# Softmax denominators spread by transfers through DRAM, and convolution steps laid over thirteen units of attention, in a diffusion-transformer layer

## The chip, the cores and the metric

The kernel runs on one core of a Trainium2 chip. The core has five engines with a queue of instructions each: TensorE (PE; its weight loads are listed apart as PEld), VectorE (DVE), ScalarE (ACT), GpSimd (POOL) and SyncE (SP, which here only issues transfers). Each queue is worked off in the order in which it was built, and engines wait for each other by semaphores. The metric is the device time of one execution in microseconds (us); lower is better.

## The reference

One layer over 1024 latent tokens of width 1024 with a context of 256 tokens: a half-step gated feed-forward network (FFN), then a short gated convolution and an attention in parallel, merged by gates and a projection, then a second FFN. Everything is float32. The change is in the attention and in the convolution's projection `y_conv @ w_bc`, which runs beside it.

```python
def gqa_attend(q, k, v):
    s = jnp.einsum('btkgd,blkd->bkgtl', q, k, preferred_element_type=jnp.float32) * (HEAD_DIM ** -0.5)
    p = jax.nn.softmax(s, axis=-1).astype(v.dtype)
    return jnp.einsum('bkgtl,blkd->btkgd', p, v)

def merge_branches(y_conv, o_attn, gate_logits, w_bc, w_ba, w_out):
    g_conv, g_attn = jnp.split(jax.nn.sigmoid(gate_logits), 2, axis=-1)
    return (g_conv * (y_conv @ w_bc) + g_attn * (o_attn @ w_ba)) @ w_out
```

There are 8 query heads and 2 key/value heads of width 128. Each of the 1024 latent queries attends in one softmax to 256 context and 1024 latent keys.

## The kernel before

To keep float32 precision, a product is made of three matmuls of a faster 32-bit form (`fp32r`): each operand is split in a high part (an ACT copy, shown as CAST) and a low part (a subtraction on DVE or POOL), and high x high, high x low and low x high are summed (`mm3`).

Attention is cut in 16 `Unit`s: 8 heads by 2 chunks of 512 queries (`C0`, `C1`). A unit has four parts.

- `begin` splits its 512 queries into two tiles `qs`.
- `scores(qt)`, for four groups of 128 queries: three 256-wide matmuls `ps<-kc,qs` against the context keys and two times three 512-wide ones `ps<-kl,qs` against the latent keys, into `ps` banks of PSUM (5 banks). DVE takes the maximum of each piece (`m`) and of the three (`nm`), ACT exponentiates the pieces into SBUF (`pc`, `pl`, `pl`) and accumulates the row sums, and DVE adds these up (`rsum`).
- `turn(kt)`, for ten groups of 128 keys: four PE transposes `pt<-ident,pc` or `pt<-ident,pl` into one `pt` bank (2 banks), which is split to a pair of tiles `pts` (CAST on ACT, subtraction on DVE).
- `values(kt)`: three matmuls `po<-pts,...` that add up over the ten groups in `po`, of which there is one bank. `po` holds head dimension by queries, so the row sums, which lie one query to a partition, have to be turned and spread over all partitions before they can divide it. That is `output`, at the end of the unit: reciprocal `rinv` on DVE, four PE transposes of `rinv` (each column spread over 128 columns) into a `pt` bank, a copy of `po` to SBUF on ACT (`q<-po`), and a multiplication on DVE (`q<-q,pt`).

The main loop (L1635) runs for unit 1 to 15. It makes the scores of one unit, and between them it takes steps from two generators: `rest` (`seconds()`: the turns and values of all units in order, with values three groups behind the turns) and `fill` (`fillers()`: the convolution projection in steps of three matmuls `ps<-y,wc`, 107 yields with the loads of its weights and inputs). A `conv_out` loads its gate `g`, multiplies it with the result on DVE and stores it to DRAM as `zd`. Of ten `rest` steps in a unit, with n = 3, 2, 3, 2 between the scores, each is followed by a `fill` step until the fourth score is made, and each n = 2 gives one more: 3 + 3 + 3 + 1 = 10 fill steps for each unit, so that the fillers end in unit 11. `split_output` splits finished heads into `oh` and `ol` for the merge that follows.

The order on each engine isn't the order of this code alone: when the program is built, a scheduler places the instructions by its own estimate of times, with the order in the code as the priority (except where a load or matmul is `pinned`). Moving a step in the code can so move the whole queue. Tiles come from pools with a fixed number of buffers, and an instruction waits until the buffer it writes is free: `qs`, `g`, and other 512-wide tiles share 11 buffers named `t`. All engine instructions are recorded at one line (L88, a helper), so rows of the profile are told apart by the names of tiles.

Of the kernel before, what the change touches and what calls it, by code (L numbers as in the profile page):

```python
# [9 lines left out]
F32 = mybir.dt.float32  # L10
# [8 lines left out]
P = 128  # L19
# [30 lines left out]
def tile_dit_layer(  # L50
# [44 lines left out]
    act, dve, pool, pe, sp = (Engine(e) for e in (nc.scalar, nc.vector, nc.gpsimd, nc.tensor, nc.sync))  # L95
# [7 lines left out]
    dram = ctx.enter_context(tc.tile_pool(name="dram", bufs=1, space=DRAM))  # L103
# [3 lines left out]
    def uniq(s):  # L107
        n_tiles[0] += 1
        return f"{s}_{n_tiles[0]}"

    def atile(name, shape=(P, SLOT), dt=F32):
        return apool.tile(list(shape), dt, tag="A", name=uniq(name))

    def ttile(name, n=512, dt=F32):
        t = tpool.tile([P, 512], dt, tag="t", name=uniq(name))
        return t[:, :n]

    def small(name, n, dt=F32):
        return spool.tile([P, n], dt, tag=f"s{n}_{name}", name=uniq(name))

    def ps_s(n=512):
        return psum.tile([P, 512], F32, tag="s", name=uniq("ps"), bufs=5)[:, :n]

    def ps_t(n=512):
        return psum.tile([P, 512], F32, tag="t", name=uniq("pt"), bufs=2)[:, :n]
# [10 lines left out]
    def transpose(out, in_, pinned=False):  # L136
        n = in_.shape[0]
        inst = pe.transpose(out, in_, ident[:n, :n])
        if pinned:
            tc.keep_in_program_order(inst)  # L140
# [35 lines left out]
    def col(name, k=0):  # L176
        o = voff[name] + k
        return cols[:, o : o + 1]
# [40 lines left out]
    def mm3(ps, terms, k0=0, k1=None):  # L219

        last = len(terms) - 1
        for i, (wh, wl, xh, xl) in list(enumerate(terms))[k0:k1]:
            matmul(ps, wh, xh, start=(i == 0), stop=False)
            matmul(ps, wh, xl, start=False, stop=False)
            matmul(ps, wl, xh, start=False, stop=(i == last))
# [219 lines left out]
    def run(steps, n=None):  # L445

        if n is None:
            for _ in steps:
                pass
        else:  # L450
            for _ in range(n):
                next(steps, None)
# [541 lines left out]
    def turn(toks, k, pt):  # L994
        for j, t in enumerate(toks):
            transpose(pt[:, j * P : (j + 1) * P], t[:, k * P : (k + 1) * P])
# [25 lines left out]
    pr = ttile("pr")  # L1022
# [169 lines left out]
    for j in range(NH):  # L1192
        half1.side = side(j) if j >= SIDE_FROM else None
        u, c = half1.next_first()
        v, b = half1.second(u)
# [15 lines left out]
    for d in range(0, KD, 2):  # L1211
# [3 lines left out]
        for e in range(2):  # L1215
            te = t[:, e * CT : (e + 1) * CT]
            dve.scalar_tensor_tensor(
                out=te, in0=c_acc(d + e), scalar=gate1["c"][:, d + e : d + e + 1], in1=te, op0=ALU.mult, op1=ALU.add
# [71 lines left out]
    for i in range(KD):  # L1290
        u = atile("u")
# [5 lines left out]
        for ch, bg, gc in mixed():  # L1297
# [4 lines left out]
            for j in (0, 2):  # L1302
                a, b = max(o, 1 - j), min(o + 512, L + 1 - j)
                ya = y[:, a - o : b - o]
                dve.scalar_tensor_tensor(
                    out=ya, in0=u[:, a + j - 1 : b + j - 1], scalar=col(f"w{j}", i), in1=ya, op0=ALU.mult, op1=ALU.add
# [181 lines left out]
    def split_output(hd, *chunks):  # L1488
        if o_parts[hd] is None:
            o_parts[hd] = atile("oh", dt=F32R), atile("ol", dt=F32R)  # L1490
        a, b = chunks[0][1], chunks[-1][1] + 512
        split(q_f[hd][:, a:b], *(t[:, a:b] for t in o_parts[hd]))

    class Unit:
# [11 lines left out]
        def scores(self, qt):  # L1506
            g = self.g
            qh, ql = (t[:, qt * P : (qt + 1) * P] for t in self.qs)
            if qt % 2 == 0:
                self.sx = ps_s()  # L1510
            sx = self.sx[:, (qt % 2) * CT : (qt % 2 + 1) * CT]
            parts = [(self.pc[:, qt], sx)]
            mm3(sx, [(qh, ql, k_ctx[:, 2 * g], k_ctx[:, 2 * g + 1])])
            m3, nm, rs = small("m3", 3), small("nm", 1), small("rs", 3)
            dve.reduce_max(out=m3[:, 0:1], in_=sx, axis=AX.X)
            if self.hd == 0 and self.ch[1] == 0 and qt < 2:
                pl = wpool.tile([P, SLOT], F32, tag="raw", name=uniq("pl"), bufs=3)
            else:
                pl = atile("pl")
            self.pl.append(pl)  # L1520
            for j in range(2):
                ps = ps_s()
                kh, kl = (t[:, j * 512 : (j + 1) * 512] for t in k_lat[g])
                mm3(ps, [(qh, ql, kh, kl)])
                dve.reduce_max(out=m3[:, j + 1 : j + 2], in_=ps, axis=AX.X)
                parts.append((pl[:, j * 512 : (j + 1) * 512], ps))
            dve.tensor_reduce(out=nm[:], in_=m3[:], axis=AX.X, op=ALU.max, negate=True)
            for j, (dst, ps) in enumerate(parts):
                act.activation(out=dst, in_=ps, func=AF.Exp, bias=nm[:], accum_out=rs[:, j : j + 1])
            dve.reduce_sum(out=self.rsum[:, qt : qt + 1], in_=rs[:], axis=AX.X)  # L1530

        def turn(self, kt):

# [15 lines left out]
            matmul(po, vl, pts[:, 0], start=False, stop=(kt == 9))  # L1549

        def output(self):
            rinv = small("rinv", 4)
            of = q_f[self.hd][:, self.ch[1] : self.ch[1] + 512]
            dve.reciprocal(out=rinv[:], in_=self.rsum[:])
            pr = ps_t()
            for qt in range(4):
                transpose(pr[:, qt * P : (qt + 1) * P], rinv[:, qt : qt + 1].to_broadcast([P, P]))
            act.copy(out=of, in_=self.po)
            dve.tensor_mul(out=of, in0=of, in1=pr)

    def seconds():

# [45 lines left out]
    u = units[0]  # L1608
# [26 lines left out]
    for n_unit, u in enumerate(units[1:], 1):  # L1635
        u.begin()
        for n in (3, 2, 3, 2):
            u.scores(len(u.pl))
            for _ in range(n):
                run(rest, 1)  # L1640
                if len(u.pl) < 4:
                    run(fill, 1)
            if n == 2:
                run(fill, 1)
            if n == 2 and n_unit >= 13:
                split_output(next(to_split), C0, C1)
    run(fill)
    run(rest, 4)
# [17 lines left out]
    for ch in (C0, C1):  # L1666
        o = ch[1]
        for d in range(KD):
# [7 lines left out]
                out=xs(d, ch), in0=ps, scalar=modl[:, 40 + d : 41 + d], in1=xs(d, ch), op0=ALU.mult, op1=ALU.add  # L1676
# [12 lines left out]
        out=gf[:], in0=cols[:, voff["gf"] : voff["gf"] + 8], scalar1=math.sqrt(D), scalar2=None, op0=ALU.mult  # L1689
# [96 lines left out]
    for j in range(NH):  # L1786
        if j > 1:
            run(late_steps, 3)
        u, c = fast.next_first()
        v, b = fast.second(u)  # L1790
# [79 lines left out]
```

## Time and profile before

| | |
|---|---|
| median of 3 runs | 2720.67 us (2720.63 to 2721.49) |
| the profiled execution's own time | 2717.89 us |
| its span in the profile | 2716.1 us |
| granted TensorE clock | 0.991 |
| attention in the profile | about 1486 to 1895 us |
| PE transposes `pt<-ident,rinv` | 64 |
| ACT copies `q<-po` | 16 |

The profile shows one execution. A row of a group has the operation, output and inputs (buffer numbers left out), the number of instructions, their busy time, the mean of one in ns, and the idle time of the engine just before them with what ended it. A row of the timeline has the start, the duration, the engine and the operation, and in square brackets the idle time before it. `SPq` is SP's queue, in which transfers are issued.

### The profile page before, as it was taken

What the parts mean: (1) busy time and instruction counts of PE and PEld (TensorE: products, weight loads), DVE (VectorE), ACT (ScalarE), POOL (GpSimd) and SP (SyncE); (2) the same over time, 40 slices, a digit from 0 to 9 for tenths busy, and PEclk for the clock granted to TensorE, in tenths of its full rate; (3) what the DMA queues carried; (4) which work ended last, traced back from release to release, by engine and by line L of the source; (5) the groups of instructions that cost most, each with busy time, mean ns of one, the idle gap of its engine ahead of it and who ended that gap; (6) DMA issues with size and microseconds to landing.
All of it is one profiled execution on the core that took longest, in us unless ns stands there. A gap on an engine that the chain in (4) does not pass through costs nothing.

```text
span 2716.1 us, 37388 instructions
## 1 busy us (share of the span) xinstructions
PE 2647.6 (97%) x13593; PEld 2236.8 (82%) x13593; DVE 2006.6 (74%) x3356; ACT 1167.2 (43%) x2317; POOL 532.1 (20%) x409
## 2 busy tenths in 40 slices
PE   7999899999999999999999999999999999999998
PEld 4788798888778877888999888877888888888888
DVE  5889666988787899888478576685548876667885
ACT  5633443333443542333245665674226333334443
POOL 1244001221010043333033111100000442330100
PEclk9999999999999999999999999999999999999998
DMA  7665553445984345433312321001533552227831
GB/s 264 212 195 170 166 168 100 147 129 179 324 206 105 113 151 186 135 118 120 109 32 87 97 82 43 28 32 47 175 105 124 179 163 93 86 89 283 183 86 63
DMA packets 369922, 364.85 MB, mean 134 GB/s; under 512 B 27831, under 2 KB 261449, under 8 KB 369737
## 3 DMA queue, kind: packets, MB, share of 16 engines
q1 hardware_dynamic: 360712, 345.17, 38.5%
q0 software_dynamic: 9024, 17.30, 4.0%
q8 instruction: 106, 1.74, 0.3%
q14 instruction: 80, 0.65, 0.1%
HBM read 296.30 MB, written 66.06 MB: 133 GB/s over the span
## 4 chain that ended last, share of the span: by engine, by line
PE 55%; DVE 3%; ACT 1%; issue 0%; DMA 0%; DVEq 0%; ACTq 0%
PE ps L88 45%; PE pt L88 5%; PE po L88 4%; DVE xb L88 0%; DVE ol L88 0%; ACT pts L88 0%; DVE pts L88 0%; DVE wl L88 0%; DVE x L88 0%; DVE r L88 0%; ACT pl L88 0%; DMA y<-yd 0%; ACT q L88 0%; ACT oh L88 0%; DVE t L88 0%
## 5 line engine op out<-in xcount | busy, mean ns | idle before, releaser
L88 PE MATMUL ps<-r,wl 128*128 128x512 f32 x5232 | 1208.9, 391 | 14.9 <-ACT wl L88 7.9
L88 PEld LDWEIGHTS ps<-r,wl 128*128 128x128 f32 x5232 | 979.8, 188 | 223.1 <-ACT wl L88 10.0
L88 ACT CAST wl<-raw 128x512 fp32r<-128x512 f32 x286 | 176.9, 620 | 291.2 <-PE ps L88 191.6
L88 POOL TENSOR_TENSOR s<-raw 128x512 f32<-128x512 f32 x64 | 95.5, 1492 | 1011.0 <-DMA raw<-in_ffn_w_in_dram 641.7
L88 ACT CAST wl<-s 128x512 fp32r<-128x512 f32 x256 | 158.0, 620 | 315.1 <-PE ps L88 233.4
L88 DVE TENSOR_TENSOR wl<-raw,wl 128x512 fp32r<-128x512 f32 x284 | 198.6, 700 | 80.8 <-ACT wl L88 77.0
L88 DVE TENSOR_TENSOR wl<-s,wl 128x512 fp32r<-128x512 f32 x256 | 230.3, 900 | 12.6 <-ACT wl L88 11.6
L88 POOL TENSOR_TENSOR s<-raw,s 128x512 f32<-128x512 f32 x64 | 107.3, 1677 | 355.2 <-DVE wl L88 347.3
L88 DVE SCALAR_TENSOR_TENSOR macc<-rawm,silu_c,macc 128x512 f32<-128x512 f32 x168 | 141.0, 855 | 8.5 <-DMA rawm<-in_w_mod_dram 7.4
L88 PE MATMUL ps<-wh,r 128*128 128x256 f32 x768 | 141.6, 285 | 0.0
L88 DVE TENSOR_TENSOR pts<-pt,pts 128x512 fp32r<-128x512 f32 x160 | 108.8, 687 | 39.3 <-ACT pts L88 38.3
L88 DVE TENSOR_REDUCE m<-ps 128x1 f32<-128x512 f32 (+1 forms) x192 | 110.9, 596 | 31.1 <-PE ps L88 30.3
L88 DVE TENSOR_TENSOR u<-u,ps 128x512 f32<-128x512 f32 x168 | 114.1, 679 | 23.2 <-PE ps L88 22.9
L88 ACT CAST pts<-pt 128x512 fp32r<-128x512 f32 x160 | 93.2, 593 | 88.6 <-PE pt L88 86.7
L88 PE MATMUL ps<-rh,wl 128*128 128x512 f32 x360 | 123.7, 395 | 3.9 <-ACT rh L88 3.9
L88 ACT CAST rh<-hid 128x512 fp32r<-128x512 f32 x132 | 81.0, 620 | 103.4 <-PE ps L88 86.3
L88 PEld LDWEIGHTS ps<-wh,r 128*128 128x128 f32 x768 | 120.6, 192 | 0.0
L88 ACT CAST wh<-raw 128x512 fp32r<-128x512 f32 (+1 forms) x88 | 69.4, 796 | 100.5 <-PE ps L88 73.0
L88 PE MATMUL po<-pts,vh 128*128 128x512 f32 x256 | 110.6, 438 | 1.5 <-ACT pts L88 1.5
L88 PE MATMUL ps<-wl,r 128*128 128x256 f32 x384 | 108.8, 283 | 0.0
L88 DVE TENSOR_TENSOR rl<-hid,rh 128x512 fp32r<-128x512 f32 x132 | 89.9, 686 | 23.8 <-ACT rh L88 11.4
L88 PE MATMUL ps<-kl,qs 128*128 128x512 f32 x384 | 105.3, 397 | 0.0
(295 smaller groups left out, 5082.0 us busy)
## 6 DMA issues: line engine op xcount, KB each, us to landing
raw<-in_ffn_w_in_dram SPq DMA_DIRECT2D x125, 512.0 KB
raw<-in_ffn_w_out_dram SPq DMA_DIRECT2D x72, 512.0 KB
rawm<-in_w_mod_dram SPq DMA_DIRECT2D x128, 256.0 KB
raw<-in_w_in_dram SPq DMA_DIRECT2D x61, 512.0 KB
hid<-hd SPq DMA_DIRECT2D x40, 512.0 KB
ws<-in_ffn_w_out_dram POOLq DMA_DIRECT2D x30, 512.0 KB, 6.6
ucd<-uc SPq DMA_DIRECT2D x22, 512.0 KB
hd<-c SPq DMA_DIRECT2D x38, 256.0 KB
```

What stands on the lines that cost most here:

```text
L88: inst = getattr(self.engine, name)(*args, **kw)
```

## The change

Two things are changed. First, the reciprocal of the row sums is made right after the fourth score group, and is spread by two transfers on SP: `rinv` (128 partitions by 4) is stored in DRAM as a row of 512 numbers (`rd<-rinv`), and this row is loaded to all 128 partitions (`pr<-rd`, 128 x 512) into a `t` buffer. `output` becomes one DVE multiplication that reads `po` in PSUM and `pr` in SBUF (`q<-po,pr`). The four transposes and the ACT copy of a unit go. Second, the first `rest` step behind a score group with n = 3 takes no fill step any more: 2 + 3 + 2 + 1 = 8 fill steps for each unit, so that the fillers end in unit 13; and `split_output` is called at other places of units 14 and 15 (three times in each, instead of twice in units 13, 14 and 15).

```diff
@@ -1528,6 +1528,14 @@
             for j, (dst, ps) in enumerate(parts):
                 act.activation(out=dst, in_=ps, func=AF.Exp, bias=nm[:], accum_out=rs[:, j : j + 1])
             dve.reduce_sum(out=self.rsum[:, qt : qt + 1], in_=rs[:], axis=AX.X)
+            if qt == 3:
+                rinv, rd = small("rinv", 4), dram.tile([1, 4, P], F32, name=uniq("rd"))
+                self.pr = ttile("pr")
+                dve.reciprocal(out=rinv[:], in_=self.rsum[:])
+                sp.dma_start(out=rd[0].rearrange("a p -> p a"), in_=rinv[:])
+                sp.dma_start(
+                    out=self.pr.rearrange("p (a b) -> p a b", b=P), in_=rd[:].to_broadcast([P, 4, P])
+                )
 
         def turn(self, kt):
 
@@ -1549,14 +1557,8 @@
             matmul(po, vl, pts[:, 0], start=False, stop=(kt == 9))
 
         def output(self):
-            rinv = small("rinv", 4)
             of = q_f[self.hd][:, self.ch[1] : self.ch[1] + 512]
-            dve.reciprocal(out=rinv[:], in_=self.rsum[:])
-            pr = ps_t()
-            for qt in range(4):
-                transpose(pr[:, qt * P : (qt + 1) * P], rinv[:, qt : qt + 1].to_broadcast([P, P]))
-            act.copy(out=of, in_=self.po)
-            dve.tensor_mul(out=of, in0=of, in1=pr)
+            dve.tensor_mul(out=of, in0=self.po, in1=self.pr)
 
     def seconds():
 
@@ -1636,13 +1638,13 @@
         u.begin()
         for n in (3, 2, 3, 2):
             u.scores(len(u.pl))
-            for _ in range(n):
+            for i in range(n):
                 run(rest, 1)
-                if len(u.pl) < 4:
+                if (i or n == 2) and len(u.pl) < 4:
                     run(fill, 1)
             if n == 2:
                 run(fill, 1)
-            if n == 2 and n_unit >= 13:
+            if n_unit >= 14 and len(u.pl) > 1:
                 split_output(next(to_split), C0, C1)
     run(fill)
     run(rest, 4)
```

The built queues show where the scheduler then puts things. The examples are from unit 6, whose first `po` matmul is the first row with a new `po` tile.

PE before, at the first `po` matmul of unit 6 (`po_15901`). `qs_16038` and `qs_16039` are queries of unit 8, `rinv` belongs to the end of unit 5:

```order
L88 MATMUL ps_16197<-kl_12130,qs_16039 128x512
L88 MATMUL pt_15860<-ident,rinv_15858 128x128 x4
L88 MATMUL ps_16256<-kl_12130,qs_16038 128x512
L88 MATMUL ps_16256<-kl_12131,qs_16038 128x512
L88 MATMUL ps_16256<-kl_12130,qs_16039 128x512
L88 MATMUL ps_16261<-kl_12130,qs_16038 128x512
L88 MATMUL ps_16261<-kl_12131,qs_16038 128x512
L88 MATMUL ps_16261<-kl_12130,qs_16039 128x512
L88 MATMUL po_15901<-pts_15818,vc_11847 128x512 x3
L88 MATMUL po_15901<-pts_15829,vc_11847 128x512 x3
```

Here the last score matmuls of unit 6 stand far ahead of this piece; those of unit 8 are just being made.

PE in the changed kernel, at the first `po` matmul of unit 6 (`po_15840`). `ps_15698<-kl,qs` is the last score of unit 6, `pc_15493` its exponentials against the context, `po_15592` belongs to unit 5:

```order
L88 MATMUL po_15592<-pts_15730,vh_11844 128x512
L88 MATMUL po_15592<-pts_15730,vl_11846 128x512
L88 MATMUL ps_15698<-kl_12128,qs_15489 128x512
L88 MATMUL ps_15698<-kl_12129,qs_15489 128x512
L88 MATMUL ps_15698<-kl_12128,qs_15490 128x512
L88 MATMUL pt_15769<-ident,pc_15493 128x128
L88 MATMUL pt_15780<-ident,pc_15493 128x128
L88 MATMUL po_15840<-pts_15774,vc_11847 128x512
L88 MATMUL pt_15794<-ident,pl_15503 128x128
L88 MATMUL pt_15794<-ident,pl_15568 128x128
L88 MATMUL pt_15794<-ident,pl_15630 128x128
L88 MATMUL pt_15794<-ident,pl_15692 128x128
```

The last score of unit 6 now stands two transposes ahead of the unit's first `po` matmul, and the transposes of its third tile, from `pl`, directly behind.

ACT before, at the first CAST that unit 6's `po` needs (`pts_15818`). `pl_16000` belongs to unit 7, `pc_16042` and `pl_16052` to unit 8, and the `pts` ahead of it to unit 5:

```order
L88 ACTIVATE pl_16000,rs_15998<-ps_16006,nm_15997 128x512
L88 CAST pts_15724<-pt_15719 128x512
L88 CAST pts_15761<-pt_15756 128x512
L88 ACTIVATE pc_16042,rs_16050<-ps_16044,nm_16049 128x256
L88 ACTIVATE pl_16052,rs_16050<-ps_16053,nm_16049 128x512
L88 ACTIVATE pl_16052,rs_16050<-ps_16058,nm_16049 128x512
L88 CAST pts_15772<-pt_15767 128x512
L88 CAST pts_15818<-pt_15813 128x512
L88 CAST wc_16080<-raw_16079 128x1024
L88 CAST pts_15829<-pt_15824 128x512
```

In the changed kernel (`pts_15774`; `pc_15493` and the two `pl` are unit 6's last group of scores):

```order
L88 CAST wc_15608<-raw_15607 128x1024
L88 ACTIVATE pc_15493,rs_15690<-ps_15622,nm_15689 128x256
L88 ACTIVATE pl_15692,rs_15690<-ps_15693,nm_15689 128x512
L88 ACTIVATE pl_15692,rs_15690<-ps_15698,nm_15689 128x512
L88 CAST pts_15774<-pt_15769 128x512
L88 CAST pts_15785<-pt_15780 128x512
L88 CAST qs_15739<-q_12863 128x512
```

The exponentials ahead of the CAST were those of later units and are now those of the same unit's last score group.

SP in the changed kernel, around units 5 and 6:

```order
L88 DMA pr_15460<-rd_15459 128x512
L88 DMA g_15614<-gcd 128x512
L88 DMA zd<-g_15614 128x512
L88 DMA raw_16423<-in_w_branch_conv_dram 128x8x128
L88 DMA rd_15709<-rinv_15708 128x4x1
L88 DMA pr_15710<-rd_15709 128x512
L88 DMA g_15867<-gcd 128x512
L88 DMA zd<-g_15867 128x512
L88 DMA raw_16727<-in_w_branch_conv_dram 128x8x128
```

The pair `rd`, `pr` of each unit stands among the loads of gates `g` and weights `raw` and the stores `zd`; the load `pr` waits until the store `rd` has landed, and what stands behind it waits on SP with it.

## The prediction, made before the run

> **What bounds the kernel now.** I read the page first, then the attention stretch by windows and groups, then the timeline at the places where the order of instructions changes. The first line of the page is the busy time of each engine:
>
> ```profile
> PE 2647.6 (97%) x13593; PEld 2236.8 (82%) x13593; DVE 2006.6 (74%) x3356; ACT 1167.2 (43%) x2317; POOL 532.1 (20%) x409
> ```
>
> TensorE (PE) is the bound. A change gains what it takes off PE's queue or out of PE's waits, and loses what it adds there. Attention takes 1486 to 1895 us; by windows (columns: stretch, length, then busy us and count of PE, PEld, DVE, ACT, POOL):
>
> ```profile
> 1486.00:1804.00 318.00, 316.25 (x1717) 265.64 (x1716) 216.24 (x466) 204.81 (x514) 43.28 (x26) 1.00 0.19 60
> 1804.00:1895.00 91.00, 85.83 (x474) 68.89 (x473) 58.48 (x99) 49.44 (x100) 0.00 (x0) 1.00 0.12 38
> ```
>
> While scores and convolution steps last, PE is idle for 1.75 us in 318; in the tail, where only turned and multiplied tiles remain, for 5.2 in 91. Matmuls overlap, so work has to be counted by the distance of starts. Three links of the chain give it:
>
> ```profile
> 1512.09 7.21 PE ps L88 x33
> 1594.88 0.87 PE pt L88 x8
> 1878.65 1.39 PE po L88 x6
> ```
>
> That is 0.109 us for a transpose (0.87/8) and 0.23 for a 512-wide matmul (1.39/6; 7.21 holds 256-wide score matmuls too, at about 0.12). A 512-wide matmul is shown busy for some 0.4, so each PE gap hides another 0.17: the tail's 5.2 us in about 15 gaps are some 7.8 us of lost PE time, and before 1804 one gap of 1.2 and one of 0.5 matter (others are in the unchanged part). About 10 us of waits could go at most.
>
> **Removed.** The groups of the attention stretch (busy us, mean ns, idle before):
>
> ```profile
> L88 PE MATMUL pt<-ident,rinv 128*128 128x128 f32 x64 | 9.6, 272 | 0.0
> L88 ACT COPY q<-po 128x512 f32<-128x512 f32 x16 | 9.6, 603 | 9.3 <-PE po L88 9.3
> L88 DVE TENSOR_TENSOR q<-q,pt 128x512 f32<-128x512 f32 x16 | 11.0, 684 | 5.6 <-PE pt L88 5.5
> ```
>
> The 64 `rinv` transposes lie on PE: 64 x 0.109 = **-7.0 us**. The 16 copies on ACT (9.6 us) are covered by PE and give nothing by themselves. The 16 DVE multiplications stay but now read `po` directly, so DVE, not ACT, frees the only `po` bank. Before, that hand-off looks like this:
>
> ```profile
> 1600.24 0.59 ACT L88 COPY q<-po 128x512 f32<-128x512 f32 x1
> 1600.89 1.20 PE L88 MATMUL po<-pts,vc 128*128 128x512 f32 x4 [0.32 <-ACT q L88]
> ```
>
> The bank is free again 0.65 us after the copy starts; with a DVE multiplication of 0.68 it is 0.74, so 0.1 us more where PE stands at it.
>
> **Moved.** The new order of the PE queue is the large term. Before, ten filler calls for each unit make the scheduler let scores run ahead: between the last score matmul of a unit and its first `po` matmul stand, in the order, 9.0, 11.5, 16 and 23 us of PE work for units 0 to 3 and 32 to 48 for units 4 to 15. The trace agrees:
>
> ```profile
> L88 PE MATMUL pt<-ident,rinv x64: 270/272/275, 1548.0 to 1881.8; 128*128 128x128 f32 x64
> L88 DVE RECIPROCAL rinv<-rsum x16: 168/178/180, 1516.7 to 1829.8; 128x4 f32<-128x4 f32 x16
> ```
>
> The first reciprocal (all scores of unit 0 exponentiated) precedes the first `rinv` transposes (end of unit 0) by 31 us, the last by 52: a unit takes 409/16 = 26, so the lead grows from 5 us to a whole unit. With the new layout the scores lead by nearly nothing. The same cover, counted in the new order at 0.227, 0.118 and 0.109 us, is for units 0 to 15: 5.89, 0.55, 0.55, 2.12, 0.55, 2.46, 0.44, 1.45, 4.40, 2.48, 8.40, 3.24, 1.23, 1.23, 2.12, 3.24 us. In ACT's queue the first CAST of the unit (`pts<-pt`, needed by the first `po` matmul) stands directly behind the three exponentials of the last row group.
>
> What must pass between that last score matmul and the first `po` matmul, from rows:
>
> ```profile
> 1515.58 0.52 PE L88 MATMUL ps<-kc,qs 128*128 128x256 f32 x3
> 1516.13 0.42 DVE L88 TENSOR_REDUCE m<-ps 128x1 f32<-128x256 f32 x1 [1.63 <-PE ps L88]
> 1514.34 0.16 DVE L88 TENSOR_REDUCE nm<-m 128x1 f32<-128x3 f32 x1
> 1514.54 0.47 ACT L88 ACTIVATE pc<-ps,nm 128x256 f32<-128x256 f32 x1 [0.29 <-DVE nm L88]
> ...
> 1827.66 0.48 ACT L88 ACTIVATE pc<-ps,nm 128x256 f32<-128x256 f32 x1
> 1828.12 0.69 ACT L88 ACTIVATE pl<-ps,nm 128x512 f32<-128x512 f32 x1
> 1828.78 0.70 ACT L88 ACTIVATE pl<-ps,nm 128x512 f32<-128x512 f32 x1
> 1829.44 1.06 ACT L88 CAST oh<-q 128x1024 fp32r<-128x1024 f32 x1
> 1830.38 1.10 ACT L88 CAST pts<-pt 128x512 fp32r<-128x512 f32 x2
> 1831.02 1.29 DVE L88 TENSOR_TENSOR pts<-pt,pts 128x512 fp32r<-128x512 f32 x2 [1.05 <-ACT pts L88]
> 1831.04 0.50 PE L88 MATMUL po<-pts,vh 128*128 128x512 f32 x1 [1.21 <-ACT pts L88]
> 1831.77 0.66 PE L88 MATMUL pt<-ident,pl 128*128 128x128 f32 x4 [0.22 <-DVE pts L88]
> ```
>
> Last start of the three score matmuls to the maximum 0.33 (1516.13 less 1515.82), maximum 0.42, then 0.04 and 0.20 to the start of `pc`, three exponentials 1.78 (1829.44 less 1827.66), CAST 0.59, 0.05 to PE: **3.4 us** where the context scores come last, 3.8 where a 512-wide matmul and its 0.68 us maximum do, and about 1.05 more where a weight or `oh` CAST stands between (1829.44 to 1830.38 shows 0.94). The rows at 1831 are the very event: PE waits 1.2 us at a `po` matmul because ACT has exponentials and an `oh` CAST ahead of the CAST it needs. Nothing behind it on PE can run.
>
> Chain less cover, unit by unit: units 1, 2, 4: 2.9 each (8.7); unit 6: 3.4; 7: 2.4; 3 and 5: 1.3 each; 12 and 13: 2.2 each; 9 and 14 (a CAST between): 2.4 each; 15: 1.3; 0 and 8: 0.8 each (the transposes of its first tile end late, then CAST); 11: 1.0 (its first `po` matmul follows unit 10's last with nothing between, so it meets the DVE multiplication); 10: 0. Sum **+30.2 us**.
>
> Behind each such wait comes another. A `pt` bank is free 1.75 us after its last transpose (0.37 to the CAST, 0.59, subtraction 0.69, hand-overs); in twelve units the order leaves 0.44 there, and since most of it passes during the first wait, about 0.5 remains (1831.04 to 1831.77 shows it: 0.73 where 0.23 is work). 12 x 0.5 = **+6.1 us**.
>
> The tail shrinks: after the last score 148 transposes (37 tiles) remained, now 44 (11 tiles), so of some 10 us of old waits about five of 0.5 stay: **-7.7 us**.
>
> **Added.** 32 transfers on SP. Nearest rows: a four-byte-element transfer of 128 elements, and the landing of a 256 KB load:
>
> ```profile
> 2307.01 1.11 SPq L88 DMA_DIRECT2D mcol<-mrow  x2
> 2311.33 0.31 DVE L88 TENSOR_TENSOR modl<-mcol,bcol 128x4 f32<-128x4 f32 x1 [2.23 <-DMA mcol<-mrow]
> ws<-in_ffn_w_out_dram POOLq DMA_DIRECT2D x6, 256.0 KB, 7.1
> ```
>
> From the last issue (2307.57) to its use are 3.8 us; 512 elements cost between that and four times that (15), the broadcast 7.1: 11 to 22 us, I take 11 (elements spread over the same 16 engines). `pr` is wanted a unit later, about 26 us, so nothing is waited for in units 0 to 14; in the last, 30 value matmuls (6.8 us), 36 transposes (3.9) and their waits leave 12 to 15, so 0 to +8. I take 0. While SP waits for the first transfer to land, loads of `g`, weights `raw`, `y` and stores `zd` queue behind it for up to 4 to 15 us; the fillers that use them come a call or more later. `pr` also holds one of 11 `t` buffers, so the next unit's `qs` CAST may wait on a store of `g`; 0 to +0.5 a unit, and I take 0.
>
> Sum: -7.0 + 30.2 + 6.1 - 7.7 = **+21.6 us** on the profiled run's 2717.89, that is 2739.5; the median of the runs shown, 2720.67, is 2.8 above that run, so **2742**.
>
> The Trainium skill ("PSUM — Partial Sum Buffer", section "Engine vs sequencer instructions") says that matmuls start and complete in program order and that the queues of ACT, DVE and POOL are strict first-in-first-out. By it the +36 us stand; if matmuls could pass a waiting one, the sum would be -14.7, rival 1. The trace agrees: at 1831.04 and at 1600.89 no later matmul started in the gap.
>
> **Rivals.**
>
> 1. *Faster: the waits at unit starts don't come.* Then -7.0 - 7.7 give 2706. It is one mechanism: whether ACT gets to the first CAST while PE still has work. It decides when the waits with their bank waits are under 14.7 - 5.4 = 9.3 us instead of 36. For it: DVE and ACT are idle a third of the stretch. Against it: the maximum needs the last score, whatever is idle, and the cover is counted. 0.06.
> 2. *About the same: the waits are half as long.* At 10 to 20 us they cancel the gains: 2716 to 2726. For it: ACT catches up in each wait, so the waits on score banks that follow vanish. Against it: those cost under 2 us before 1804. 0.08.
> 3. *Slower still: queues behind the wait.* If at each of 15 starts ACT or DVE has 0.5 to 1 us of other work ahead (copies or multiplications of the unit before, a `qs` CAST), that is +8 to +15: 2749 to 2756. For it: the gap of 1.2 us at 1582.96, where ACT was dense. 0.16.
> 4. *The transfers are late.* At 22 us or more `pr` is missed in the last unit (+8, 2749), and with SP blocked a `g` now and then. The point is a pair time above the rest of unit 15, 12 to 15 us. 0.10.
>
> The Trainium skill ("DMA: Bandwidth & Descriptors", section "Specifications") says that under 512 B the engines do a read-modify-write; the store of 512 four-byte elements is all such pieces, which speaks against the change. By its fit ("Anatomy of one DMA", 2.0 us plus bytes over 436 GB/s) the pair would take an estimated 4.6 us, less than my rows give. Only rival 4 hangs on it; the trace has the landing of a like transfer in 3.8 us.
>
> **Chances.** The forecast 0.60, rivals as above (0.40). The forecast's own range, with chains of 3.2 to 4 us, is 2734 to 2749. The range 2727 to 2758 adds rivals 3 and 4 and leaves out 1 and 2 and a little above. 0.2% is 5.4 us, about what a measurement of this kernel can tell from no change: faster (below 2715) is rival 1, 0.06; same is rival 2, 0.08; slower 0.86.
>
> **What would show it.** In the profile of the changed kernel: no `pt<-ident,rinv`; PE idle before 1804 up from 1.75 us to over 25, ended by `ACT pts`, once a unit at its first `po<-pts,vc`; a second, shorter wait on `DVE pts` behind it; PE nearly full in the tail; no long idle of DVE ended by the transfer of `pr`. It is wrong if the waits at `po<-pts,vc` sum to under 15 us, if DVE's `q<-po,pr` waits for a transfer, or if PE waits elsewhere.

## The result: 2.5% slower

The changed kernel takes 2790.48 us (median of 4 runs, 2783.53 to 2794.08) against 2720.98 before on the same chip: ratio 1.0254, 95% interval 1.024 to 1.0268. Forecast were 2742, in a range up to 2758. The sign is right; the loss is 69.5 us instead of 21. The profiled execution took 2793.1 us (span 2791.3).

The busy times of the page, and the clock that PE was granted by fortieths of the span:

```profile
PE 2671.4 (96%) x13529; PEld 2246.1 (80%) x13529; DVE 2008.0 (72%) x3356; ACT 1159.8 (42%) x2301; POOL 531.3 (19%) x409
PEclk9999999999999999999999899999999999999998
```

PE has 64 instructions less and is busy for 24 us *longer*. That can't be work: an instruction is busy for longer at a lower clock, and the clock's row has an 8 inside attention. The windows of the attention stretch (columns as before; the number behind the counts is the granted clock, then DMA):

```profile
1486.00:1804.00 318.00, 282.85 (x1411) 229.20 (x1410) 179.89 (x376) 160.91 (x399) 37.35 (x26) 0.94 0.20 57
1520.00:1550.00 30.00, 20.52 (x99) 16.41 (x97) 12.39 (x26) 10.52 (x24) 3.64 (x2) 0.83 0.23 54
1800.00:1825.00 25.00, 15.13 (x74) 12.18 (x72) 7.43 (x18) 7.57 (x21) 3.68 (x2) 0.80 0.18 53
```

In 318 us PE now runs 1411 matmuls where it ran 1717, and idles for 35.2 us where it idled for 1.75. Two places are worst, near 1530 and near 1815. Everything behind attention takes as long as before, and the unchanged part ahead of it took 3.1 us longer in this execution.

**A unit start.** The timeline where unit 1 begins (PE, ACT and DVE rows):

```profile
1552.11 0.51 PE L88 MATMUL ps<-kc,qs 128*128 128x256 f32 x3
...
1552.97 0.41 DVE L88 TENSOR_REDUCE m<-ps 128x1 f32<-128x256 f32 x1
...
1553.61 0.47 ACT L88 ACTIVATE pc<-ps,nm 128x256 f32<-128x256 f32 x1 [0.92 <-DVE nm L88]
...
1554.23 0.44 PE L88 MATMUL pt<-ident,pc 128*128 128x128 f32 x2 [1.40 <-ACT pc L88]
...
1555.40 1.08 ACT L88 CAST pts<-pt 128x512 fp32r<-128x512 f32 x2
...
1556.05 0.79 PE L88 MATMUL po<-pts,vc 128*128 128x512 f32 x1 [1.38 <-ACT pts L88]
...
1556.77 1.11 PE L88 MATMUL pt<-ident,pl 128*128 128x128 f32 x4
```

This is the forecast's chain. PE stands twice, once for the exponentials (its transposes need `pc`) and once for the CAST, and a third time for the `pt` bank: the last row starts 0.72 behind the one above it, 0.5 more than the length of a 512-wide matmul at full clock. Half of that 0.5 is already the clock, which the trace records at 0.50 from 1555.4. And the last rows are slow: four transposes take 1.11 us where they took 0.60 to 0.66.

**A late `g`.** The worst place, on SP, DVE and PE:

```profile
1520.16 0.37 SPq L88 DMA_DIRECT2D rd<-rinv  x1
...
1529.87 0.33 SPq L88 DMA_DIRECT2D pr<-rd  x1
1530.26 0.42 SPq L88 DMA_DIRECT2D g<-gcd  x1
...
1535.10 0.69 DVE L88 TENSOR_TENSOR g<-g,ps 128x512 f32<-128x512 f32 x1 [10.88 <-DMA g<-gcd]
...
1535.85 1.22 PE L88 MATMUL ps<-kl,qs 128*128 128x512 f32 x2 [8.05 <-DVE g L88]
```

From the issue of the store of 512 four-byte elements 9.7 us pass until SP issues `pr`. The load of `g` is queued behind and needs another 4.8 us until DVE can start; DVE (in order) stands at the multiplication with `g` for 10.9 us with its maxima and subtractions queued behind it, and PE waits 8 us for a `ps` bank that this multiplication would free. It happens again at 1818.54, in unit 10, with 9.9 us. In all of attention SP waits for the store in each of the 16 units (us in total, times, longest):

```profile
SPq L88 <- DMA rd<-rinv: 133.1, 16, 9.4
```

**The clock in that gap**, in windows of 2 us:

```profile
1526.00:1528.00 2.00, 1.80 (x10) 1.15 (x9) 0.00 (x0) 0.59 (x1) 0.14 (x1) 1.00 0.00 0
1532.00:1534.00 2.00, 0.00 (x0) 0.00 (x0) 0.00 (x0) 0.00 (x0) 0.00 (x0) 0.50 0.96 201
1538.00:1540.00 2.00, 2.00 (x6) 1.58 (x6) 0.98 (x3) 0.54 (x1) 0.00 (x0) 0.50 0.00 0
1542.00:1544.00 2.00, 2.00 (x15) 1.68 (x13) 1.48 (x4) 1.45 (x4) 0.00 (x0) 1.00 0.00 0
```

PE works again from 1536, but at 0.50 until 1541.7: 6 matmuls in 2 us, then 15. (Eight of the 15 are short transposes. Like for like, the next matmul starts 0.43 us behind the `po<-pts,vl` at 1538.14 and 0.23 us behind the one at 1541.99.)

**The account.** I take each distance between the starts of two consecutive matmuls in attention less its length at full clock (0.227, 0.118 and 0.109 us). What is over is put to the clock (up to one more length) where the trace records a clock of 0.50, else it is a wait if above 0.15 us.

| first score matmul after 1486 to last `po` matmul, us | before | changed | difference |
|---|---|---|---|
| total | 404.3 | 476.7 | +72.4 |
| work at full clock | 387.0 | 380.4 | -6.6 |
| lost to half clock (half-clock windows) | 0.0 (0) | 19.2 (10) | +19.2 |
| waits over 0.15 us | 10.6 | 69.3 | +58.7 |
| the rest | 6.8 | 7.9 | +1.1 |

A half-clock window is a stretch that the trace's clock record puts at 0.50. Of the waits, the 16 unit starts make 32.4 (sum over the starts), the `pt` bank behind them 13 times 0.3 to 0.5, about 6.2, the two late `g` 18.3; about 12.4 are elsewhere. The two half-clock windows of 10 us stand at the two late `g`; the other eight (3.4 or 6.8 us each) stand at unit starts.

Which eight of the 16 starts get one doesn't follow from the waits alone: units 7 and 12 wait 2.2 and 2.1 us, and only 7 gets a half-clock window. All changes in the clock record lie on one grid of 3.41 us. In the ten grid steps that end with a fall of the clock PE was busy, by the spans that the trace shows, for 0 to 0.61 of the step (for 1.27 us of the 3.4 from 1552.0, for instance). The four emptiest steps without a fall had 0.53 to 0.61. So PE needn't be idle for a whole step to lose the clock. That a start is spared where the edge of a step cuts its waits fits this, but wasn't tried.

### The profile page after: what moved, and what is told of

Its sections match the earlier page's. It is cut to its first block, busy times and chain, and to the rows that moved or that the text cites. A ratio compares the mean times of both kernels' runs of the same rounds, so it can differ in the third digit from the quotient of the medians.

```text
span 2791.3 us, 37300 instructions
## 1 busy us (share of the span) xinstructions
PE 2671.4 (96%) x13529; PEld 2246.1 (80%) x13529; DVE 2008.0 (72%) x3356; ACT 1159.8 (42%) x2301; POOL 531.3 (19%) x409
## 5 line engine op out<-in xcount | busy, mean ns | idle before, releaser
L88 POOL TENSOR_TENSOR s<-raw 128x512 f32<-128x512 f32 x64 | 95.1, 1486 | 926.0 <-DMA raw<-in_ffn_w_in_dram 527.3
L88 ACT CAST wh<-raw 128x512 fp32r<-128x512 f32 (+1 forms) x88 | 69.5, 796 | 111.7 <-PE ps L88 76.4
L88 DVE TENSOR_TENSOR rl<-hid,rh 128x512 fp32r<-128x512 f32 x132 | 90.4, 690 | 23.4 <-ACT rh L88 10.9
```

The lines of the kernel that those rows point to most:

```text
L88: inst = getattr(self.engine, name)(*args, **kw)
```

## The experiments

Theory A: the scores lose their lead because `pr` takes one of the `t` buffers that the next units' `qs` come from. Theory B: the filler layout takes it, as the prediction said. Theory C: the store that blocks SP is the main cost. Each run is told by its ratio to the kernel before on the same chip, with the 95% interval; that kernel's median moved between 2719.4 and 2721.0.

**1. The layout alone** (the old reciprocal; only the loop of the change, with its places of `split_output`):

```diff
-            for _ in range(n):
+            for i in range(n):
                 run(rest, 1)
-                if len(u.pl) < 4:
+                if (i or n == 2) and len(u.pl) < 4:
...
-            if n == 2 and n_unit >= 13:
+            if n_unit >= 14 and len(u.pl) > 1:
```

> Only the second part of the change: 8 filler steps a unit, the old reciprocal with transposes. Theory A (the scores lose their lead because pr sits in the ring of 11 t buffers): the lead stays (9 to 47 us of PE work between a unit's last score and its first po matmul in the built order), no waits at unit starts, 2713 to 2728 us. Theory B (the filler layout takes the lead, as the prediction said): 2760 to 2790 us. Theory C (the store rd that blocks SP costs most): about 2720, as A.

Measured: 2722.63 us, ratio 1.0009 (0.9999 to 1.0018). Attention has 11.9 us of waits (10.6 before) and two half-clock windows that cost some 3 us. In its trace the lead is there: between the last score matmul of a unit and its first `po` matmul lie 8.7 to 46.9 us of PE work, against 8.7 to 48.0 before and 0.2 to 8.3 in the change. The layout alone takes neither the lead nor a time that can be told from nothing, and the prediction's cause is false.

**2. The transfers alone** (the old loop, the rest as in the change):

```diff
-            for i in range(n):
+            for _ in range(n):
                 run(rest, 1)
-                if (i or n == 2) and len(u.pl) < 4:
+                if len(u.pl) < 4:
...
-            if n_unit >= 14 and len(u.pl) > 1:
+            if n == 2 and n_unit >= 13:
```

> Only the first part of the change: reciprocal by transfers with pr in a t buffer, the old 10 filler steps a unit. Theory A: the lead is lost (0.4 to 8.5 us in the built order), 2765 to 2800 us with waits on ACT at unit starts and half-clock windows. Theory B: the lead stays, 2705 to 2730 us. Theory C: 2735 to 2760 us, its loss mostly waits of DVE for g.

Measured: 2794.89 us, ratio 1.0275 (1.0259 to 1.029): the whole loss, with 70.2 us of waits and 21.1 of half clock. B falls. C isn't told apart by this one, since late `g` is 16.1 of it.

**3. `pr` in another pool.** The whole change, with one name changed:

```diff
-                self.pr = ttile("pr")
+                self.pr = atile("pr", (P, 512))[:]
```

> The whole change, but pr takes a buffer of the large A pool instead of one of the 11 t buffers. Built order: 9 to 30 us of PE work between a unit's last score and its first po matmul. Theory A: waits on ACT at unit starts are gone, and what SP's block of 8 to 10 us a unit costs stays: 2715 to 2740 us, of which about 5 if the lead also hides late g loads (then about 2710). Theory B: about as the change, 2770 to 2795. Theory C: 2735 to 2765, since the store still blocks SP.

Measured: 2728.36 us, ratio 1.0028 (1.0017 to 1.0038). The unit starts are gone: 62 of the 69 us come back while SP is blocked as before. What stays are waits of 19.7 us and 4.6 of half clock, and they show what SP's block costs with the lead there:

```profile
SPq L88 <- DMA rd<-rinv: 126.4, 15, 9.8
...
1598.63 0.33 SPq L88 DMA_DIRECT2D pr<-rd  x1
1599.06 3.92 SPq L88 DMA_DIRECT2D y<-yd  x6
...
1605.36 0.62 ACT L88 CAST y<-y 128x512 fp32r<-128x512 f32 x1 [8.03 <-DMA y<-yd]
...
1607.43 0.79 PE L88 MATMUL po<-pts,vh 128*128 128x512 f32 x1 [6.17 <-ACT pts L88]
```

(The first row is the total of SP's waits for the store to land, their number and the longest.) Six loads of `y` are queued behind the pair, ACT stands 8 us at the first, and PE 6.2 behind ACT.

**4. Also fewer, larger pieces.** `rinv` is stored as it lies, 16 bytes a partition, and DVE reads `pr` in permuted order:

```diff
-                sp.dma_start(out=rd[0].rearrange("a p -> p a"), in_=rinv[:])
+                sp.dma_start(out=rd[0].rearrange("(p a) -> p a", a=4), in_=rinv[:])
...
-            dve.tensor_mul(out=of, in0=self.po, in1=self.pr)
+            v = lambda t: t.rearrange("p (a b) -> p a b", a=4)
+            dve.tensor_mul(out=v(of), in0=v(self.po), in1=self.pr.rearrange("p (b a) -> p a b", a=4))
```

> As the run before with pr in the A pool, and in addition rinv is stored as 128 pieces of 16 bytes instead of 512 of 4 (the multiplication on DVE reads pr in permuted order). Theory A with the block counted apart: the store lands in 3 to 5 us instead of 8 to 10, so g loads are less late: 0 to 20 us below the run before, best case about 2706 (7 us of transposes and some tail waits less than before the change). If the landing time does not fall, it is not the number of pieces that makes it long, and the time is that of the run before.

Measured: 2712.87 us, ratio 0.9975 (0.9962 to 0.9989): a quarter of a per cent faster than the kernel before, 15.5 us below run 3. SP's waits for the store:

```profile
SPq L88 <- DMA rd<-rinv: 20.4, 16, 2.0
```

How the 2 KB are cut sets the landing: from the issue of `rd` to that of `pr` pass 1.4 to 2.4 us here with 128 pieces, 8.0 to 9.8 in the change with 512. The number of the pieces, their size and their order in DRAM changed together, so which of these counts isn't shown. It isn't the moving of the pieces that the trace records: where nothing else is queued, the last of the 512 small packets starts 1.3 us behind the issue, the last of the 128 1.0 us behind. Between that packet and the issue of `pr` lie 6.9 to 8.6 us with 512 pieces and 0.4 to 1.4 with 128, and what fills them the trace doesn't show. Attention has no half-clock window and is 9.2 us shorter than before: 6.6 us of transposes and 2.5 of waits (8.1 are left).

**5. Small pieces without the lead.** `pr` back in a `t` buffer, 128 pieces:

> The whole change with pr still in a t buffer, but rinv stored as 128 pieces of 16 bytes. The lead is lost as in the change (0.4 to 8.4 us in the built order). Theory A1 (the long landing of the store, by blocking SP, makes g late, beside the lost lead): the waits of DVE for g (18 us of PE waits and two of the half-clock windows of 10 us) go, the unit-start waits stay: 2762 to 2772 us. Theory A2 (late g is a result of the lost lead alone): 2783 to 2795. Theory D (the unit-start waits themselves come from the late pr): below 2745.

Measured: 2787.39 us, ratio 1.0244 (1.0231 to 1.0257), which can't be told from the change itself. Late `g` falls from 18.3 us to 3.0 as A1 said, but the time doesn't: waits in all fall from 69.3 to 62.6 only, half clock stays at 20.2. Other waits grew: those of transposes for `pc` from 7.2 to 12.9 us, those ended by `nm`, `rsum` and the `qs` CAST by 4.6 together. The built order differs a little too (chain less cover is about 1 us more in sum). A1's size is refuted. How much of the 15 us was only hidden by the starts and how much the other order took stays open.

**6. The pair on POOL's queue** (`pool.dma_start` for both, 512 pieces, `pr` in a `t` buffer):

> The whole change with pr in a t buffer and 512 pieces of 4 bytes, but both transfers issued from POOL's queue, so SP is not blocked. Theory A1: the store lands as late as before, but g is on time: 2760 to 2778 us, less if POOL's subtractions for qs and wc are not delayed by its own waits, more if they are. If it stays at 2783 to 2795, it is not SP's block that makes g late.

Measured: 2878.23 us, ratio 1.0572 (1.0557 to 1.0587), far outside every expectation. Waits by engine:

```profile
POOL pr L88 <- DMA rd<-rinv: 98.3, 11, 11.6
PE ps L88 <- POOL qs L88: 64.4, 15, 8.0
```

PE has no more long wait for `g` (one of 1.0 us), but POOL now stands at the landing, and behind it waits the subtraction that makes the low half of the next unit's `qs`. With no lead, PE needs it at once: 15 waits of up to 8 us, and 25 half-clock windows (44.5 us).

**7. A buffer of its own** (128 pieces, no memory added):

```diff
-    tpool = ctx.enter_context(tc.tile_pool(name="tpool", bufs=11))
+    tpool = ctx.enter_context(tc.tile_pool(name="tpool", bufs=10))
...
-                self.pr = ttile("pr")
+                self.pr = tpool.tile([P, 512], F32, tag="pr", name=uniq("pr"), bufs=1)[:]
```

> 16-byte pieces; pr gets one buffer of its own and the t pool has 10 instead of 11, so that no memory is added. Built lead 9 to 36 us. If the lead was lost because pr takes its turn among the t buffers, and not for want of a buffer: 2705 to 2718 us, like the run with pr in the A pool (2712.9). If it was want of a buffer: over 2740.

Measured: 2747.74 us, ratio 1.0104 (1.0091 to 1.0118), which by the total would speak against A. The trace says where: attention begins at 1517.1 instead of 1487.4 us and takes 402.7, 1.6 less than before. Ten `t` buffers cost some 30 us in the phases ahead of it; in attention the lead is there, and no half-clock window.

**8. Run 4 with the old layout:**

> pr in the A pool, 16-byte pieces, and the old layout of 10 filler steps a unit. Theory A: the layout is worth little by itself (2722.6 against 2719.4 in its own run): 2706 to 2718 us, within 6 us of the run with the new layout (2712.9). Theory B (the layout costs or gains in its own right): more than 8 us away from 2712.9.

Measured: 2712.74 us, ratio 0.9971 (0.996 to 0.9982), 0.1 us from run 4. The layout is worth nothing with the lead either.

**9. `pr` in a `t` buffer, taken later.** Against run 5 (128 pieces, the new layout) only the place in the code changes:

```diff
 # scores, qt == 3
-                self.pr = ttile("pr")
-                sp.dma_start(out=self.pr, in_=rd[:].to_broadcast([P, 4 * P]))
+                self.rd = rd
 # values
             if kt == 0:
                 self.po = ps_o()
+                self.pr = ttile("pr")
+                sp.dma_start(out=self.pr, in_=self.rd[:].to_broadcast([P, 4 * P]))
```

> pr is again one of the 11 t buffers, and the layout is that of the change; only the place in the code moves where pr's buffer is taken and loaded: from the end of the scores to the first values call of the unit (16-byte pieces). In the built order the CAST of the next unit's qs, which in the change stands 3 to 6 rows behind the last exponentials of the unit before, stands far ahead of them again, and the lead is 9 to 40 us. Theory E (the buffer of pr, taken in the program ahead of the next unit's qs from the same pool, holds qs back until the reciprocal is there): 2705 to 2718 us. Theory F (a pr in the t pool costs time whenever it is taken): over 2740.

Measured: 2711.29 us, ratio 0.9963 (0.9951 to 0.9976), the lowest median, though it can't be told from runs 4 and 8; against run 5 the two moved lines are worth 76 us. So `pr` in the `t` pool costs nothing when its buffer is asked for at the unit's first values call, which in the code comes after the `begin` of the next unit, so that `qs` gets its buffers first. In this trace the CAST of the next unit's `qs` is again 22 to 36 ACT instructions ahead of the last exponentials of the unit before. (`pr` is also held for a shorter time so, and no run tells the two fully apart. Run 7 speaks for the order: there one buffer less is left for all the rest, and the lead stays.) The windows of this run:

```profile
1486.00:1804.00 318.00, 316.05 (x1711) 265.59 (x1710) 218.37 (x468) 196.98 (x504) 42.63 (x26) 1.00 0.24 67
```

PE idles for 2.0 us in 318, as before the change (1.75).

**10. The same with 512 pieces:**

> The same with 512 pieces of 4 bytes, as in the change; the PE order is nearly the same, the load of pr stands right behind the store on SP in most units, and so SP waits 8 to 10 us a unit. If SP's block costs time by itself once the lead is there: 5 to 18 us above the run with 16-byte pieces, by late y, wc or g loads. If the lead hides it: within 4 us of that run.

Measured: 2723.24 us, ratio 1.0008 (0.9999 to 1.0017), 12 us above run 9. SP waits again:

```profile
SPq L88 <- DMA rd<-rinv: 136.8, 16, 9.8
ACT y L88 <- DMA y<-yd: 12.4, 2, 7.9
```

With the lead, SP's block costs 12 to 15 us (run 10 less 9, run 3 less 4), and in both runs ACT stands some 8 us at a late `y`; without the lead (run 5 against the change) it can't be told from nothing.

**11. The change, with PE kept busy in the wait.** One of the transposes behind a unit start is repeated:

```diff
-                transpose(pt[:, qt * P : (qt + 1) * P], src)
+                for _ in range(11 if (kt, qt) == (1, 3) else 1):
+                    transpose(pt[:, qt * P : (qt + 1) * P], src)
```

> The change itself, with the transpose of the last query group of each unit's second tile done eleven times instead of once (same result): 10 more transposes a unit, 1.09 us, on PE inside the wait for the first po matmul, 17.4 us of PE work in all. Theory G (the half-clock windows come from the idle time of PE and cost time of their own, 19 us in the change): the added work is hidden at 12 or 13 starts (3 to 5 us not hidden), the number of half-clock windows in attention falls from 10 to 6 or fewer and 6 to 12 us come back: 2778 to 2789 us. Theory H (the windows have another cause or cost nothing beside the waits): still 9 to 12 windows, 2790 to 2800 us.

Measured: 2793.78 us, ratio 1.0269 (1.0254 to 1.0284). Half of G holds: windows of half clock in attention fall from 10 to 4, their loss from 19.2 to 7.6 us, and the clock is full in a stretch of unit starts (first row; in the change it is 0.97 there), while the two late `g` keep theirs (second row):

```profile
1700.00:1750.00 50.00, 45.67 (x250) 37.37 (x248) 28.50 (x62) 26.17 (x69) 4.03 (x3) 1.00 0.17 41
1800.00:1825.00 25.00, 15.18 (x76) 12.35 (x75) 7.99 (x18) 7.43 (x18) 3.70 (x2) 0.80 0.18 53
```

The total didn't fall. Of the 17.5 us added, 10.9 went into the wait for the CAST (18.4 to 7.5), but waits for `pc` grew by 9.5; in the account of attention the work is +17.4, the half clock -11.6, all waits some -4, and the sum +2.9. That idle time of PE brings the half clock is shown; that its 19 us would come back one for one isn't, since other waits grew while the half clock went.

The trace also says what counts as busy. In the grid steps from 1632.7 and 1690.7, at the starts of units 4 and 6, PE ran nothing but transposes except for 2 and 4% of the step, for 0.47 and 0.49 of it in all, and the clock stayed full. At the same starts of the change, with 0.13 and 0.19, it fell.

## Why the prediction was wrong

**The unit starts were right in place and size.** The step "chain less cover, unit by unit" gave 30.2 us, the trace has 32.4: units 1 and 2 3.1 each (2.9), unit 6 3.3 (3.4), unit 7 2.3 (2.4), units 12 and 13 2.1 (2.2), unit 10 none (0). The largest miss is unit 4, 4.3 (2.9), with a wait of 2.8 at a transpose of `pc`. The `pt` bank was about 6.2 (6.1). The transposes were -6.6 (-7.0). Reading covers from the built order works.

**The cause given for them was wrong.** "Before, ten filler calls for each unit make the scheduler let scores run ahead ... with the new layout the scores lead by nearly nothing": run 1 and run 8 show that the layout does neither. It is the place of `pr`'s buffer (runs 2, 3, 9). The sign of it stood in the rows quoted ahead of the prediction: in ACT's new order, `CAST qs_15739`, which makes unit 7's queries, stands right behind the first CASTs of unit 6. Scores can't lead if `qs` doesn't. In the traces that CAST is 2 to 5 ACT instructions behind the last exponentials of the unit before in the change, and 32 to 140 ahead of them before it. That the pool gives buffers out in the order of the code, so that `qs` of the next unit can't be placed before `pr` is, fits runs 3, 7 and 9, but the scheduler's rule itself wasn't tried.

**The sum missed 51 us, 47 of them in three terms.** It had 21.6 for attention, and 72.4 were measured. Of the signs of being wrong that it named, the last came: PE waits elsewhere.

- *Half clock, +19.2, not in the sum.* The prediction priced waits by their length alone. The kernel before has no half-clock window in attention, so no row quoted there shows one; its clock record has nine stretches at 0.50 elsewhere, and the prediction didn't look at them.
- *Late `g`, +18.3, taken at 0.* The step is "the fillers that use them come a call or more later". SP's block was named and its victim too, but bounded (4 to 15 us) and then set to nothing, with no number for what would hide it. The landing was also taken too low, 11 us for the pair with under 4 for the store; the store alone took 8.0 to 9.8. Rival 4 had this at 0.10, with a price of 8 us in the last unit; it came in units 0 and 10.
- *Other waits, +9.5.* "The tail shrinks ... -7.7" was true of the tail's own waits, but other waits came in mid-unit, where PE waits for a `pt` bank that DVE frees only after a maximum (6.0 us, nine times) and for score banks that ACT frees (3.2).

With these and the 2 us more at the starts the sum comes to 71. Rival 3 (queues behind the wait, +8 to +15) has the third term's size, but put it at the starts. Rival 1 is near what came of the change with `pr` taken late and small pieces: 2711 in run 9, where it gave 2706.

**Two rules beside the rows.** That matmuls start in program order held: no later matmul started in the gaps of 8.05 and 9.87 us. The Trainium skill ("TensorE: Matmul & The Clock Gate", section "What's actually happening") says that a monitor halves PE's clock by windows of 3413 ns in which PE was idle, and that a busy window restores it. The trace agrees in the lengths: the half-clock stretches in attention last 3.41, 6.83 or 10.24 us, all at 0.50. It doesn't agree that PE has to be idle for a whole window: the clock fell behind windows in which PE was busy for up to 0.61. So the prediction's waits of up to 3.4 us at unit starts should have had a price for the clock too. The read-modify-write under 512 bytes that the Trainium skill names ("DMA: Bandwidth & Descriptors", section "Specifications") doesn't tell the slow store from the fast one by itself: 16-byte pieces fall under it too and landed in 1.4 to 2.4 us. That is near the fixed 2.0 us that the same page of the Trainium skill gives (section "Anatomy of one DMA"), though for transfers issued by GpSimd, while these are SP's; the prediction's estimate of 4.6 us for the pair rests on it, and with 512 pieces the store alone took more.

## What to carry to other kernels

A buffer taken from a pool in program order is a place in a queue: before adding a tile that waits long for its content, look what comes behind it from the same pool, and take the buffer as late as its use allows. Price waits of PE with a second term for the clock wherever they leave it idle for about half of some 3.4 us, even in two parts, and price a blocking transfer by what is queued behind it on its issuing queue, with the landing taken from a transfer cut into the same pieces and not from the bytes. When a change with two parts loses, run each part alone first: one of the two here was worth nothing, and the other gained 7 to 10 us instead of losing 70 after two lines were moved (or `pr` was given another pool) and the store had fewer pieces.

## What was not expected of the hardware

- A store of 2 KB in 512 pieces of 4 bytes held its queue for 8.0 to 9.8 us (the change), in 128 pieces of 16 bytes for 1.4 to 2.4 (run 4), though its recorded packets had all started within 1.3 and 1.0 us where nothing else was queued.
- Two waits of 1.5 us with some work between were enough to halve PE's clock for 3.4 or 6.8 us. A half-clock window cost 1.8 to 1.9 us on the mean (44.5/25 in run 6; 19.2/10).
- Transposes kept the clock up: PE at full clock behind a step of 3.41 us with 0.47 of transposes and little else (run 11).
